# A gated-attention and Hyena block on one core: opening by quarters over three weight blocks, another order around both layer norms, the second norm's shift formed on TensorE, full-width inverse transforms

## The chip, the cores and the metric

The kernel runs on one core of a Trainium2 chip. The metric is the device time of one execution in microseconds (us): 1901.46 us, the median of three runs (1899.14 to 1902.49). Beside the runs there is one profiled execution, whose trace gives the rows shown below. About 0.2% is what separates two kernels from no difference here.

## The reference

One encoder block on x of 256 tokens by 2048 channels, in float32. Two branches (a gated linear attention in both directions, and a Hyena branch whose convolutions are done by transforms) are merged by gates, projected, and normed; a feed-forward layer and a second norm follow.

```python
proj = h @ w_in[l]
q, k, v, r, af, ab, hy_u, gate_logits = jnp.split(proj, split_idx, axis=-1)
...
merged = g[:, :, 0, :] * (y_gla @ w_gla_o[l]) + g[:, :, 1, :] * (y_hy @ w_hy_o[l])
mix = merged @ w_out[l]
h = _layernorm(DEEPNORM_ALPHA * h + mix, ln1_g[l], ln1_b[l])
ff = jnp.square(jax.nn.relu(h @ w_ff1[l])) @ w_ff2[l]
h = _layernorm(DEEPNORM_ALPHA * h + ff, ln2_g[l], ln2_b[l])
```

with, in `_layernorm`, `(xf - mu) * rsqrt(var + eps) * g + b`. In the Hyena branch each of two orders computes `zf = rfft(z)`, multiplies by the filter's spectrum, and transforms back (`irfft`).

## The kernel before, in words

**Products.** Every weight matrix is cut by the host into blocks of 128 x 2048 floats (1 MB). `fetch` (L89) issues the next block's DMA on SP's queue into one of three raw buffers and splits each half of it into a high part, cast on ACT to the reduced fp32 type `fp32r` (L81), and a low remainder, subtracted on DVE (L82). Three buffers each hold high and low halves. A product is formed from three matmuls, high by high, high by low and low by high. Where the weight stands still (`channel_pair`, L133), the activation's high and low parts lie side by side, so one matmul of 512 columns (L143) gives two of the three and one of 256 (L144) the third; sixteen such pairs make one block's product, in one of four "main" PSUM buffers, and ACT and DVE then add its two halves. Where the activation stands still (`token_products`, L162 to L164), each of the three is a matmul of 512 columns. Four "side" PSUM buffers serve all small work: filters, transforms, transposes.

**The opening.** x arrives transposed, in four pieces of 0.5 MB (`xr0` to `xr3`), and is split like a weight into `xT`. SP's queue carries, in this order, block 0's first half, two x pieces, block 0's second half, two x pieces, then block 1 by halves and the rest. TensorE runs three warm-up matmuls on zeros in plain fp32 (L209), then block 0's product `pa` (L370, L371), then the pairs of q. The constants for the filters (`filt_consts`, L233) are issued on ACT's queue. The first filter product is `mlp` (L255), also plain fp32.

**The inverse transform.** `hy_inv` (L648) runs 16 times. Into one side buffer it forms, for each of two token blocks, six matmuls of 256 columns with `mm3` (L221, matmuls L222 to L224).

**The layer norms.** z1 holds the 256 tokens as two token blocks (`tb` 0 and 1) of 128 x 2048. `norm_scale` (L758) aggregates the statistics and forms rs = rsqrt(var + eps) and nb = -mean * rs by some ten operations of one column. `norm_chunk` (L769) then does, chunk by chunk in the order of `CHUNKS` (L767), z * rs + nb on ACT (L772), times the row of scales (L773) and plus the row of shifts (L774) on DVE; the chunk at 1536 runs these two on POOL. The rows lie across all partitions and are loaded by `load_rows` (L733) on ACT's queue into one buffer, which both norms use in turn.

Before the first norm, the last quarter of the output projection is done token block by token block with `column_products` (L776), three matmuls of 256 columns at a time. After it, `turn` transposes each chunk (L824), except that the chunk at 1536 is transposed last, and splits it into `hT`. The first of ff1's products is done by token halves (`by_tile`), so that it can begin on token block 0's half: 16 half pairs of 256 and 128 columns.

The feed forward runs four quarters, `ff1(qi)` and `ff2(qi)`; `add_ff` (L848) adds the result to z1 and, in the last quarter, takes the statistics (L856). The last products are again `column_products` for token block 0, then for token block 1, each followed by the second norm and its stores: six per token block, on SP's queue (L884).

**What sets the order.** The instruction order on each engine comes from a scheduler at build time that simulates a timeline; `tc.high_priority` lifts the additions and statistics ahead of other work. Side work is queued with `later` and run by `pump` between blocks.

Of the kernel before, what the change touches and what calls it, by code (L numbers as in the profile page):

```python
# [16 lines left out]
P = 128  # L17
D = 2048
# [22 lines left out]
def block_kernel(  # L41
# [47 lines left out]
    def fetch(between=lambda n, h: None):  # L89
# [5 lines left out]
        if n > 1:  # L95
            nc.sync.dma_start(raw, wblk[n])
        parts = []
        for h in range(2):
            if n <= 1:
                hs = slice(h * D // 2, (h + 1) * D // 2)  # L100
                nc.sync.dma_start(raw[:, hs], wblk[n][:, hs])
                between(n, h)
            hi = wp.tile([P, D // 2], F32R, tag="whi", bufs=3, name=f"whi{n}_{h}")
            lo = wp.tile([P, D // 2], F32R, tag="wlo", bufs=3, name=f"wlo{n}_{h}")
            split_hi_lo(hi, lo, raw[:, h * 1024:(h + 1) * 1024])
            parts.append((hi, lo))
        queue.append(parts)

# [24 lines left out]
    def channel_pair(act, name, dst=None, scale=1.0, by_tile=False):  # L133
        if dst is None:
            dst = base.tile([P, 2, L], F32, tag="sum", name=f"{name}_s")
        for c in range(2):
            ps = psum_main(f"{name}_{c}").rearrange("p (a b) -> p a b", a=2)
            parts = next_block()
            for ts in ((slice(0, P), slice(P, L)) if by_tile and c == 0 else (slice(0, L),)):
                for kt in range(KT):  # L140
                    hi, lo = parts[kt // 8]
                    js = slice(kt % 8 * P, (kt % 8 + 1) * P)
                    MM(ps[:, :, ts], hi[:, js], act[:, kt, :, ts], start=(kt == 0), stop=False)  # L143
                    MM(ps[:, 0, ts], lo[:, js], act[:, kt, 0, ts], start=False, stop=(kt == KT - 1))  # L144
            low = base.tile([P, L], F32, tag="low", name=f"{name}_l{c}")
            nc.scalar.activation(low, ps[:, 1], AF.Copy, scale=scale)
            nc.vector.scalar_tensor_tensor(dst[:, c], ps[:, 0], scale, low, op0=ALU.mult, op1=ALU.add)
            pump()
        return dst
# [48 lines left out]
    with tc.tile_pool(name="xp", bufs=1) as xp:  # L198
        def load_x(n, h):
            for g in (2 * h, 2 * h + 1):  # L200
                xr = xp.tile([P, 4, L], F32, tag=f"xr{g}", name=f"xr{g}")
                nc.sync.dma_start(xr, xt[:, 4 * g:4 * g + 4, :])
                split_hi_lo(xT[:, 4 * g:4 * g + 4, 0], xT[:, 4 * g:4 * g + 4, 1], xr)

        wu = xp.tile([P, 512], F32, tag="wu", name="wu")
        nc.vector.memset(wu, 0.0)
        pw = psum_side("warm")
        for _ in range(3):
            MM(pw, wu[:, 0:P], wu, start=True, stop=True)  # L209
        fetch(load_x)  # L210
# [22 lines left out]
    def filt_consts():  # L233
        raw = fp.tile([P, 4, P], F32, tag="w4", name="dftraw")
        nc.scalar.dma_start(raw, dft_in)
        split_hi_lo(dfth, dftl, raw)
        mw = fp.tile([P, 3, P], F32, tag="mlpw", name="mlpw")
        nc.scalar.dma_start(mw, mlp_w)
        mc = fp.tile([P, 4], F32, tag="mlpc", name="mlpc")
        nc.scalar.dma_start(mc, mlp_c)  # L240
        et = fp.tile([P, L], F32, tag="emb", name="emb_sb")
        nc.scalar.dma_start(et, emb)
        nc.scalar.dma_start(ba_sb, ba)
        nc.scalar.dma_start(conv_sb, convp)
        nc.scalar.dma_start(mask_sb, mask_in)
        nc.scalar.dma_start(sgn_sb, sgn_in)
        nc.scalar.dma_start(ident, ident_in)
        fst["mw"], fst["mc"], fst["g"] = mw, mc, et
# [114 lines left out]
    as_sb = base.tile([P, L], F32R, tag="as", name="as_sb")  # L363
    pa = psum_main("pa").rearrange("p (a b) -> p a b", a=2)
    fetch()
    parts = next_block()
    for kt in range(KT):
        hi, lo = parts[kt // 8]
        js = slice(kt % 8 * P, (kt % 8 + 1) * P)
        MM(pa, hi[:, js], xT[:, kt], start=(kt == 0), stop=False)  # L370
        MM(pa[:, 0], lo[:, js], xT[:, kt, 0], start=False, stop=(kt == KT - 1))  # L371
# [9 lines left out]
    k_sb = qp.tile([P, 8, L], F32, tag="k", name="k_sb")  # L381
    for dst, nm, sc in ((q_sb, "q", 1.0 / 16.0), (k_sb, "k", 1.0)):
        for c2 in range(4):
            channel_pair(xT, f"{nm}{c2}", dst[:, 2 * c2:2 * c2 + 2, :], sc)
# [263 lines left out]
    def hy_inv(c, o):  # L648
        def run():
            yh, yl = cst.pop(("Y", c, o))  # L650
            py = psum_side(f"yp{c}{o}")
            for tb in range(NT):
                dst = py[:, tb * CW:(tb + 1) * CW]
                mm3(dst, dfth[:, 2], dftl[:, 2], yh[:, tb, 0], yl[:, tb, 0], True, False)
                mm3(dst, dfth[:, 3], dftl[:, 3], yh[:, tb, 1], yl[:, tb, 1], False, True)
            py3 = py.rearrange("p (a b) -> p a b", a=2)
            if o == 0:
                zf = hp.tile([P, NT, CW], F32, tag="zf", name=f"zf{c}")
                nc.vector.tensor_tensor(zf, py3, cst.pop(("x1", c)), op=ALU.mult)
# [107 lines left out]
    CHUNKS = ((0, 256), (256, 256), (1536, 512), (512, 512), (1024, 256), (1280, 256))  # L767

    def norm_chunk(z, rows, tb, at, n, rs, nb):  # L769
        zc = z[:, tb, at:at + n]  # L770
        eng = nc.gpsimd if at == 1536 else nc.vector
        nc.scalar.activation(zc, zc, AF.Identity, scale=rs, bias=nb)  # L772
        eng.tensor_tensor(zc, zc, rows[:, 0, at:at + n], op=ALU.mult)  # L773
        eng.tensor_tensor(zc, zc, rows[:, 1, at:at + n], op=ALU.add)  # L774
# [36 lines left out]
    for tb in range(NT):  # L811
# [23 lines left out]
    fts = {}  # L835

    def ff1(qi):
        f = act_tile(ep, "f", f"f{qi}") if qi % 2 == 0 else act_tile(base, "xT", f"f{qi}")
        for c2 in range(8):
            r = channel_pair(hT, f"f{qi}_{c2}", by_tile=(qi == 0 and c2 == 0))  # L840
# [7 lines left out]
    def add_ff(ps, tb, at, n, qi):  # L848
# [27 lines left out]
    for tb in range(NT):  # L876
# [135 lines left out]
```

## Time and profile before

| | us |
|---|---|
| runs, median (lowest to highest) | 1901.46 (1899.14 to 1902.49) |
| profiled execution, span | 1896.2 |
| TensorE busy | 1868.9 |
| DVE busy | 1313.3 |
| ACT busy | 949.7 |

The profile gives no time of its own for the profiled execution beside its span; the span is 5.3 us below the median of the runs. In the rows, PE is TensorE's matmuls, PEld its weight loads, DVE the VectorE, ACT the ScalarE, POOL the GpSimd, SP the queue of DMA issues; a "q" after an engine's name is its sequencer. A timeline row gives start, duration, engine, line, operation, out<-in, shapes, count, and in brackets the idle time before it with what ended it. Neighbouring matmuls overlap in the pipeline, so a matmul's price is the distance from one start to the next. In a table of windows the columns are the window, its length, then busy time and count for PE, PEld, DVE, ACT and POOL, the clock granted to TensorE (1.00 is full), the share of the DMA engines in use, and GB/s.

### The profile page before, as it was taken

The page shows a single profiled execution, that of the slowest core. Times are in us where ns is not written, and L with a number is a line of the kernel's source. Part 1 is how long each engine was busy: PE and PEld are TensorE (multiplying, and loading weights), DVE is VectorE, ACT ScalarE, POOL GpSimd, SP SyncE. Part 2 cuts the span into 40 slices and gives each one's busy share as a digit, 9 for nine tenths or more (in the row PEclk, how much of TensorE's full clock was granted, in tenths as well). Part 3 has the DMA queues.
Part 4 walks back from the last instruction along what each step waited for, and adds up shares of the span by engine and source line. Part 5 has one row for each costly group of instructions (what it writes and reads, how often), then busy time and mean ns, then how long its engine had stood idle before and what let it go on. Part 6 is the DMA issues. An engine that isn't in the chain of part 4 may idle for free.

```text
span 1896.2 us, 25333 instructions
## 1 busy us (share of the span) xinstructions
PE 1868.9 (99%) x10060; PEld 1601.9 (84%) x10060; DVE 1313.3 (69%) x1702; ACT 949.7 (50%) x1286; POOL 38.7 (2%) x60
## 2 busy tenths in 40 slices
PE   8999999999999999999999998999999999999996
PEld 7888888888888888888888888888888888888886
DVE  6888868874799888888556567666555554665456
ACT  5555556674555555555544444444434443443343
POOL 0000000000000000000000001000000000000001
PEclk9999999999999999999999999999999999999998
DMA  8667764435555555555555754555555555555552
GB/s 289 238 218 263 262 229 157 145 139 193 193 194 210 195 195 189 206 205 204 212 180 190 274 211 155 190 192 186 200 186 192 182 195 180 198 183 194 200 181 108
DMA packets 60583, 375.09 MB, mean 198 GB/s; under 512 B 7216, under 2 KB 10928, under 8 KB 20912
## 3 DMA queue, kind: packets, MB, share of 16 engines
q1 hardware_dynamic: 46512, 324.03, 47.7%
q0 software_dynamic: 5888, 29.36, 4.2%
q10 hardware_dynamic: 8064, 20.07, 3.1%
q8 instruction: 79, 1.29, 0.3%
q14 instruction: 40, 0.33, 0.0%
HBM read 356.66 MB, written 16.78 MB: 197 GB/s over the span
## 4 chain that ended last, share of the span: by engine, by line
PE 96%; DVE 2%; ACT 1%; DMA 0%; issue 0%; ACTq 0%; SPq 0%; DVEq 0%
PE f L143 12%; PE f L144 6%; PE g L143 6%; PE w L163 6%; PE w L164 6%; PE w L162 6%; PE ho L143 3%; PE go L143 3%; PE ux L143 3%; PE uv L143 3%; PE g L144 3%; PE uz L143 3%; PE ux L144 2%; PE uv L144 2%; PE uz L144 2%; PE go L144 2%
## 5 line engine op out<-in xcount | busy, mean ns | idle before, releaser
L82 DVE TENSOR_TENSOR wlo<-raw,whi 128x1024 fp32r<-128x1024 f32 x596 | 728.4, 1223 | 495.1 <-ACT whi L81 494.2
L81 ACT CAST whi<-raw 128x1024 fp32r<-128x1024 f32 x596 | 626.6, 1052 | 783.0 <-PE w L164 190.7
L143 PE MATMUL f<-hT,whi 128*128 128x512 f32 (+1 forms) x1040 | 360.2, 392 | 0.0
L144 PE MATMUL f<-hT,wlo 128*128 128x256 f32 (+1 forms) x1040 | 289.9, 279 | 0.0
L143 PEld LDWEIGHTS f<-hT,whi 128*128 128x128 f32 x1040 | 195.4, 188 | 42.9
L144 PEld LDWEIGHTS f<-hT,wlo 128*128 128x128 f32 x1040 | 197.2, 190 | 0.1
L164 PE MATMUL w<-whi,f 128*128 128x512 f32 x480 | 188.0, 392 | 0.0
L163 PE MATMUL w<-wlo,f 128*128 128x512 f32 x480 | 188.0, 392 | 0.0
L143 PE MATMUL g<-xT,whi 128*128 128x512 f32 x512 | 180.1, 393 | 0.0
L162 PE MATMUL w<-whi,f 128*128 128x512 f32 x480 | 169.2, 392 | 0.0
L144 PE MATMUL g<-xT,wlo 128*128 128x256 f32 x512 | 144.8, 283 | 0.0
L143 PEld LDWEIGHTS g<-xT,whi 128*128 128x128 f32 x512 | 96.0, 188 | 21.7
L162 PEld LDWEIGHTS w<-whi,f 128*128 128x128 f32 x480 | 90.2, 188 | 19.9
L164 PEld LDWEIGHTS w<-whi,f 128*128 128x128 f32 x480 | 90.3, 188 | 19.7
L163 PEld LDWEIGHTS w<-wlo,f 128*128 128x128 f32 x480 | 90.3, 188 | 19.6
L144 PEld LDWEIGHTS g<-xT,wlo 128*128 128x128 f32 x512 | 96.3, 188 | 0.3
L143 PE MATMUL uz<-xT,whi 128*128 128x512 f32 x256 | 91.8, 396 | 0.0
L143 PE MATMUL ux<-xT,whi 128*128 128x512 f32 x256 | 91.7, 396 | 0.0
L143 PE MATMUL go<-yg,whi 128*128 128x512 f32 x256 | 91.1, 397 | 0.0
L143 PE MATMUL uv<-xT,whi 128*128 128x512 f32 x256 | 90.7, 393 | 0.0
L143 PE MATMUL ho<-yh,whi 128*128 128x512 f32 x256 | 90.5, 399 | 0.0
L144 PE MATMUL ux<-xT,wlo 128*128 128x256 f32 x256 | 72.5, 283 | 0.0
(329 smaller groups left out, 3338.7 us busy)
## 6 DMA issues: line engine op xcount, KB each, us to landing
raw<-wblk SPq DMA_DIRECT2D x303, 1024.0 KB, 4.8
Td<-T POOLq DMA_DIRECT2D x16, 768.0 KB, 4.4
Tl<-Td POOLq DMA_DIRECT2D x16, 768.0 KB, 4.6
w<-w4s ACTq DMA_DIRECT2D x16, 512.0 KB, 4.9
zr<-ln_rows ACTq DMA_DIRECT2D x4, 1024.0 KB, 10.7
raw<-wblk SPq DMA_DIRECT2D x4, 512.0 KB, 7.0
xr<-xt SPq DMA_DIRECT2D x4, 512.0 KB, 6.3
dec<-decay_in ACTq DMA_DIRECT2D x8, 256.0 KB, 3.5
```

The source lines that it names most:

```text
L81: nc.scalar.copy(hi, src)
L82: nc.vector.tensor_tensor(lo, src, hi.bitcast(F32), op=ALU.subtract)
L143: MM(ps[:, :, ts], hi[:, js], act[:, kt, :, ts], start=(kt == 0), stop=False)
L144: MM(ps[:, 0, ts], lo[:, js], act[:, kt, 0, ts], start=False, stop=(kt == KT - 1))
L162: MM(pss[tb], sh, wh, start=(kt == 0), stop=False)
L163: MM(pss[tb], sh, wl, start=False, stop=False)
L164: MM(pss[tb], sl, wh, start=False, stop=(kt == KT - 1))
```

## The change

Six edits. `channel_pair` is cut into parts that are used one by one.

1. **Opening by quarters over three blocks.** Three main PSUM buffers are opened at once, for the gate ranks (block 0) and q's first two blocks. x's pieces go on ACT's queue (the first in two), the three blocks by quarters on SP's (block 0's first quarter in two). Quarter by quarter, the parts are split and each block's four pairs formed. The filter constants move from ACT's queue to POOL's.
2. **Full-width inverse transforms.** Six matmuls of 512 columns instead of twelve of 256.
3. **First norm.** The chunk at 1536 goes from POOL to DVE, chunks are 256, 256, 512, 512, 512 in order, and each is transposed as it is done.
4. **ff1's first pair by tokens.** Both blocks of the pair are open; for token block 0, block 0's two halves and block 1's first half (24 half pairs), then the same for token block 1, then block 1's second half at full width.
5. **Second norm.** `add_ff` multiplies by the row of scales right after the statistics. At the end a PSUM buffer gets identity times the row of shifts plus diagonal(nb) times the row of scales, two plain fp32 matmuls for each piece of 512 columns, and one DVE operation forms z * rs + that.
6. **Stores.** Four per token block instead of six.

```diff
-    def channel_pair(act, name, dst=None, scale=1.0, by_tile=False):
+    def channel_products(ps, act, half, kts, ts=FULL, opens=True):
+        hi, lo = half
+        for kt in kts:
+            js = slice(kt % 8 * P, (kt % 8 + 1) * P)
+            MM(ps[:, :, ts], hi[:, js], act[:, kt, :, ts], start=(kt == 0 and opens), stop=False)
+            MM(ps[:, 0, ts], lo[:, js], act[:, kt, 0, ts], start=False, stop=(kt == KT - 1))
...
+    def channel_pair_by_tokens(act, name):
+        dst = base.tile([P, 2, L], F32, tag="sum", name=f"{name}_s")
+        ps = [channel_psum(f"{name}_{c}") for c in range(2)]
+        blocks = [next_block() for _ in range(2)]
+        for ts in (slice(0, P), slice(P, L)):
+            for c, h in ((0, 0), (0, 1), (1, 0)):
+                channel_products(ps[c], act, blocks[c][h], range(8 * h, 8 * h + 8), ts,
+                                 opens=(c == 0 or ts.start == 0))
+        channel_products(ps[1], act, blocks[1][1], range(8, KT))
...
-        fetch(load_x)
+        for g in range(4):
+            pieces = 2 if g == 0 else 1
+            step = 4 // pieces
+            for i in range(pieces):
+                ks = slice(step * i, step * (i + 1))
+                nc.scalar.dma_start(xr[g][:, ks], xt[:, 4 * g + step * i:4 * g + step * (i + 1), :])
+            for b in range(OPENING):
+                for i in range(pieces if b == 0 else 1):
+                    w = 512 // (pieces if b == 0 else 1)
+                    cs = slice(512 * g + w * i, 512 * g + w * (i + 1))
+                    nc.sync.dma_start(raws[b][:, cs], wblk[b][:, cs])
+        for g in range(4):
+            pieces = 2 if g == 0 else 1
+            for b in range(OPENING):
+                if g % 2 == 0:
+                    halves_of[b] = weight_half(b, g // 2)
...
+                for i in range(n):
+                    at = 512 * (g % 2) + w * i
+                    cs = slice(512 * g + w * i, 512 * g + w * (i + 1))
+                    split_hi_lo(hi[:, at:at + w], lo[:, at:at + w], raws[b][:, cs])
+                    if b == 0:
+                        ks = slice(4 * g + step * i, 4 * g + step * (i + 1))
+                        split_hi_lo(xT[:, ks, 0], xT[:, ks, 1], xr[g][:, step * i:step * (i + 1)])
+                channel_products(open_ps[b], xT, halves_of[b], range(4 * g, 4 * g + 4))
...
-        nc.scalar.dma_start(raw, dft_in)
+        nc.gpsimd.dma_start(raw, dft_in)
...
-            for tb in range(NT):
-                dst = py[:, tb * CW:(tb + 1) * CW]
-                mm3(dst, dfth[:, 2], dftl[:, 2], yh[:, tb, 0], yl[:, tb, 0], True, False)
-                mm3(dst, dfth[:, 3], dftl[:, 3], yh[:, tb, 1], yl[:, tb, 1], False, True)
             py3 = py.rearrange("p (a b) -> p a b", a=2)
+            mm3(py3, dfth[:, 2], dftl[:, 2], yh[:, :, 0], yl[:, :, 0], True, False)
+            mm3(py3, dfth[:, 3], dftl[:, 3], yh[:, :, 1], yl[:, :, 1], False, True)
...
-    CHUNKS = ((0, 256), (256, 256), (1536, 512), (512, 512), (1024, 256), (1280, 256))
+    CHUNKS = ((0, 256), (256, 256), (512, 512), (1024, 512), (1536, 512))
...
-        eng = nc.gpsimd if at == 1536 else nc.vector
         nc.scalar.activation(zc, zc, AF.Identity, scale=rs, bias=nb)
-        eng.tensor_tensor(zc, zc, rows[:, 0, at:at + n], op=ALU.mult)
-        eng.tensor_tensor(zc, zc, rows[:, 1, at:at + n], op=ALU.add)
+        nc.vector.tensor_tensor(zc, zc, rows[:, 0, at:at + n], op=ALU.mult)
+        nc.vector.tensor_tensor(zc, zc, rows[:, 1, at:at + n], op=ALU.add)
...
-            if at < 1536:
-                turn(at, n)
-        turn(1536, 512)
+            turn(at, n)
...
                 nc.vector.bn_stats(st2[:, tb, at // 256 + i, :], zc[:, i * 256:(i + 1) * 256])
+            nc.vector.tensor_tensor(zc, zc, rows2[:, 0, at:at + n], op=ALU.mult)
...
-        for at, n in CHUNKS:
-            norm_chunk(z1, rows2, tb, at, n, rs, nb)
-            nc.sync.dma_start(out[tb * P:(tb + 1) * P, at:at + n], z1[:, tb, at:at + n])
+        dg = ep.tile([P, P], F32, tag="dg", bufs=2, name=f"dg{tb}")
+        nc.vector.tensor_scalar(dg, ident, nb, None, op0=ALU.mult)
+        for c in range(4):
+            at = c * 512
+            po = psum_side(f"lo{tb}{c}")
+            MM(po, ident, rows2[:, 1, at:at + 512], start=True, stop=False)
+            MM(po, dg, rows2[:, 0, at:at + 512], start=False, stop=True)
+            zc = z1[:, tb, at:at + 512]
+            nc.vector.scalar_tensor_tensor(zc, zc, rs, po, op0=ALU.mult, op1=ALU.add)
+            nc.sync.dma_start(out[tb * P:(tb + 1) * P, at:at + 512], zc)
```

More of the change, by code (lines that the diff above doesn't have):

```diff
@@ L87, in block_kernel, with fetch @@
     stop_at = [W_OUT_END - 3]
-    def fetch(between=lambda n, h: None):
+    def fetch():
         n = fetched[0]
@@ L94, in fetch @@
         raw = wp.tile([P, D], F32, tag="raw", bufs=3, name=f"raw{n}")
-        if n > 1:
-            nc.sync.dma_start(raw, wblk[n])
+        nc.sync.dma_start(raw, wblk[n])
         parts = []
         for h in range(2):
[L99 to L104, printed above, removed]
+            hi, lo = weight_half(n, h)
             split_hi_lo(hi, lo, raw[:, h * 1024:(h + 1) * 1024])
@@ L107, in fetch, with weight_half @@
         queue.append(parts)
+    def weight_half(n, h):
+        return (wp.tile([P, D // 2], F32R, tag="whi", bufs=3, name=f"whi{n}_{h}"),
+                wp.tile([P, D // 2], F32R, tag="wlo", bufs=3, name=f"wlo{n}_{h}"))
     side = []
@@ L131, in next_block, with channel_psum, channel_sum, channel_pair @@
         return queue.popleft()
-    def channel_pair(act, name, dst=None, scale=1.0, by_tile=False):
+    FULL = slice(0, L)
+    def channel_psum(name):
+        return psum_main(name).rearrange("p (a b) -> p a b", a=2)
+    def channel_products(ps, act, half, kts, ts=FULL, opens=True):
[4 more added lines that the diff above has]
+            MM(ps[:, 0, ts], lo[:, js], act[:, kt, 0, ts], start=False, stop=(kt == KT - 1))
+    def channel_sum(dst, ps, name, scale=1.0):
+        low = base.tile([P, L], F32, tag="low", name=name)
+        nc.scalar.activation(low, ps[:, 1], AF.Copy, scale=scale)
+        nc.vector.scalar_tensor_tensor(dst, ps[:, 0], scale, low, op0=ALU.mult, op1=ALU.add)
+    def channel_pair(act, name, dst=None, scale=1.0):
         if dst is None:
@@ L136, in channel_pair @@
         for c in range(2):
-            ps = psum_main(f"{name}_{c}").rearrange("p (a b) -> p a b", a=2)
+            ps = channel_psum(f"{name}_{c}")
             parts = next_block()
[L139 to L147, printed above, removed]
+            for h in range(2):
+                channel_products(ps, act, parts[h], range(8 * h, 8 * h + 8))
+            channel_sum(dst[:, c], ps, f"{name}_l{c}", scale)
+            pump()
+        return dst
+    def channel_pair_by_tokens(act, name):
[7 more added lines that the diff above has]
+        channel_products(ps[1], act, blocks[1][1], range(8, KT))
+        for c in range(2):
+            channel_sum(dst[:, c], ps[c], f"{name}_l{c}")
             pump()
@@ L195, in block_kernel @@
     qp = qkg.enter_context(tc.tile_pool(name="qp", bufs=1))
+    OPENING = 3
+    open_ps = [channel_psum(f"open{b}") for b in range(OPENING)]
     with tc.tile_pool(name="xp", bufs=1) as xp:
[L199 to L203, printed above, removed]
         wu = xp.tile([P, 512], F32, tag="wu", name="wu")
@@ L209, in block_kernel @@
             MM(pw, wu[:, 0:P], wu, start=True, stop=True)
-        fetch(load_x)
+        raws = [wp.tile([P, D], F32, tag="raw", bufs=3, name=f"raw{b}") for b in range(OPENING)]
+        fetched[0] = OPENING
+        xr = [xp.tile([P, 4, L], F32, tag=f"xr{g}", name=f"xr{g}") for g in range(4)]
+        halves_of = [None] * OPENING
+        for g in range(4):
[14 more added lines that the diff above has]
+                    halves_of[b] = weight_half(b, g // 2)
+                hi, lo = halves_of[b]
+                n = pieces if b == 0 else 1
+                w, step = 512 // n, 4 // n
+                for i in range(n):
[6 more added lines that the diff above has]
+                channel_products(open_ps[b], xT, halves_of[b], range(4 * g, 4 * g + 4))
     ba_sb = base.tile([P, 2, 8], F32, tag="ba", name="ba_sb")
@@ L234, in filt_consts @@
         raw = fp.tile([P, 4, P], F32, tag="w4", name="dftraw")
-        nc.scalar.dma_start(raw, dft_in)
+        nc.gpsimd.dma_start(raw, dft_in)
         split_hi_lo(dfth, dftl, raw)
         mw = fp.tile([P, 3, P], F32, tag="mlpw", name="mlpw")
-        nc.scalar.dma_start(mw, mlp_w)
+        nc.gpsimd.dma_start(mw, mlp_w)
         mc = fp.tile([P, 4], F32, tag="mlpc", name="mlpc")
-        nc.scalar.dma_start(mc, mlp_c)
+        nc.gpsimd.dma_start(mc, mlp_c)
         et = fp.tile([P, L], F32, tag="emb", name="emb_sb")
[L242 to L247, printed above, removed]
+        nc.gpsimd.dma_start(et, emb)
+        nc.gpsimd.dma_start(ba_sb, ba)
+        nc.gpsimd.dma_start(conv_sb, convp)
+        nc.gpsimd.dma_start(mask_sb, mask_in)
+        nc.gpsimd.dma_start(sgn_sb, sgn_in)
+        nc.gpsimd.dma_start(ident, ident_in)
         fst["mw"], fst["mc"], fst["g"] = mw, mc, et
@@ L363, in block_kernel @@
     as_sb = base.tile([P, L], F32R, tag="as", name="as_sb")
[L364 to L371, printed above, removed]
+    pa = open_ps[0]
     a_low = base.tile([P, L], F32, tag="low", name="a_low")
@@ L381, in block_kernel @@
     k_sb = qp.tile([P, 8, L], F32, tag="k", name="k_sb")
+    for c in range(2):
+        channel_sum(q_sb[:, c], open_ps[1 + c], f"q0_l{c}", 1.0 / 16.0)
+        pump()
+    for _ in range(2):
+        fetch()
     for dst, nm, sc in ((q_sb, "q", 1.0 / 16.0), (k_sb, "k", 1.0)):
-        for c2 in range(4):
+        for c2 in range(1 if nm == "q" else 0, 4):
             channel_pair(xT, f"{nm}{c2}", dst[:, 2 * c2:2 * c2 + 2, :], sc)
@@ L839, in ff1 @@
         for c2 in range(8):
-            r = channel_pair(hT, f"f{qi}_{c2}", by_tile=(qi == 0 and c2 == 0))
+            r = (channel_pair_by_tokens if qi == 0 and c2 == 0 else channel_pair)(hT, f"f{qi}_{c2}")
             nc.vector.scalar_tensor_tensor(r, r, 0.0, r, op0=ALU.max, op1=ALU.mult)
```

## The prediction

> **What bounds the kernel now.** I read the page's shares first, then its chain of waits.
>
> ```profile
> span 1896.2 us, 25333 instructions
> PE 1868.9 (99%) x10060; PEld 1601.9 (84%) x10060; DVE 1313.3 (69%) x1702; ACT 949.7 (50%) x1286; POOL 38.7 (2%) x60
> PE 96%; DVE 2%; ACT 1%; DMA 0%; issue 0%; ACTq 0%; SPq 0%; DVEq 0%
> ```
>
> TensorE is busy for 99% of the span and carries 96% of the chain. So time can come only from what TensorE is given to do, from the few stretches in which it waits, or from a lower clock. The list of its waits and the windows of its clock come next.
>
> ```profile
> PE ht L824 <- DVE zr L774: 5.3, 3, 3.3
> PE pa L370 <- DVE xT L82: 3.4, 1, 3.4
> ```
>
> ```profile
> 2.00:6.00 4.00, 4.00 (x6) 1.33 (x4) 0.00 (x0) 1.50 (x2) 0.00 (x0) 1.00 0.84 229
> 10.00:13.00 3.00, 2.85 (x9) 2.47 (x10) 2.54 (x3) 2.34 (x3) 0.00 (x0) 0.50 1.04 386
> 1165.00:1167.00 2.00, 0.60 (x4) 0.40 (x4) 1.61 (x5) 2.00 (x4) 0.76 (x1) 1.00 0.00 0
> 1167.00:1173.00 6.00, 2.74 (x14) 2.52 (x12) 5.78 (x10) 2.24 (x6) 2.30 (x2) 0.50 0.23 86
> 1886.00:1897.00 11.00, 0.00 (x0) 0.00 (x0) 5.12 (x9) 2.02 (x4) 3.06 (x2) 0.50 0.30 95
> ```
>
> The third number of a row is PE's busy time, the third from the end the clock granted to it. Three places hold all that the change can win: the opening, where products start late and at half clock; the first layer norm, where PE idles 1.40 us in one window and 3.26 in the next, and then works at 0.50; and the end, where PE has no work left. Every matmul added elsewhere lengthens the span by its own duration.
>
> **The opening.**
>
> ```profile
> 5.79 1.04 ACT L81 CAST whi<-raw 128x1024 fp32r<-128x1024 f32 x1 [2.36 <-DMA raw<-wblk]
> 13.33 1.05 ACT L81 CAST xT<-xr 128x1024 fp32r<-128x1024 f32 x1 [0.32 <-DMA xr<-xt]
> 10.15 0.79 PE L370 MATMUL pa<-xT,whi 128*128 128x512 f32 x1 [3.36 <-DVE xT L82]
> 13.42 0.40 PE L370 MATMUL pa<-xT,whi 128*128 128x512 f32 x1
> 13.77 0.39 PE L370 MATMUL pa<-xT,whi 128*128 128x512 f32 x1
> 27.45 0.70 PE L255 MATMUL mlp<-emb_sb,mlpw 33*128 33x256 f32 x2
> 28.07 0.39 PE L144 MATMUL q<-xT,wlo 128*128 128x256 f32 x1
> ```
>
> A weight tile's pair of products (512 and 256 columns) starts every 0.35 us at full clock (13.42 to 13.77). Before, the 48 pairs of the first three blocks start at 10.15; with 16.9 us of pairs, about 1.6 lost to the half clock and 0.62 of the filter product they end near 29.25. ACT's casts follow the landings: 0.5 MB at 5.79, 3.0 MB at 13.33, five steps of 1.5 us, so some 0.33 MB/us.
>
> After, the same 5 MB come as quarters. ACT issues the five x pieces, SP twelve weight pieces and one more, and the casts stand on ACT in the order: block 0's first quarter with x's, blocks 1 and 2 with x's second and third, block 0's second quarter, x's fourth, block 1's second quarter. In front of them on ACT stand those five issues; the filter constants leave that queue for POOL's, where the later stores of T queue behind them. The first products need only 0.25 MB to land; I put them at 8.5 us. Sixteen pairs (three first quarters, one second) last 5.6 us, to 14.2. Block 1's second quarter then stands behind the cast of x's last quarter, which asks for about 3.1 MB, so 13.5 to 14; with four splits still to pass through ACT and DVE I start it at 16.8. From there eight quarter-blocks of 1.41 us run without a wait: 16.8 + 11.3 + 0.6 = 28.7. Gain 0.5. Bounds: with no wait at all, 8.5 + 16.9 + 0.6 = 26.0, a gain of 3.2; with x and weights sharing the rate evenly, x's last quarter would be behind 4 MB and the end near 30.8, a loss of 1.6.
>
> **The inverse transforms.**
>
> ```profile
> 523.37 0.28 PE L223 MATMUL yp<-Yl,dfth 128*128 128x256 f32 x1
> 524.20 0.28 PE L224 MATMUL yp<-Yh,dftl 128*128 128x256 f32 x1
> 1851.37 0.40 PE L163 MATMUL w<-wlo,f 128*128 128x512 f32 x1
> 1852.53 0.39 PE L162 MATMUL w<-whi,f 128*128 128x512 f32 x1
> ```
>
> From the first yp row to the second are seven steps, 0.119 us each; from the first w row to the second five, 0.232 each. A call has twelve of the narrow ones (1.42 us) and will have six wide ones (1.39): 0.035 us in each of 16 calls, a gain of 0.6 (0.3 to 0.9 by the rounding of the rows).
>
> **The first layer norm.**
>
> ```profile
> 1162.90 0.34 PE L143 MATMUL f<-hT,whi 128*128 128x256 f32 x1
> 1163.14 0.33 PE L143 MATMUL f<-hT,whi 128*128 128x256 f32 x1
> 1165.00 0.92 DVE L773 TENSOR_TENSOR zr<-zr 128x256 f32<-128x256 f32 x2 [0.67 <-ACT zr L772]
> 1166.90 2.76 DVE L773 TENSOR_TENSOR zr<-zr 128x512 f32<-128x512 f32 x2 [0.32 <-ACT zr L772]
> 1169.58 0.68 DVE L774 TENSOR_TENSOR zr<-zr 128x512 f32<-128x512 f32 x1
> 1171.52 0.41 DVE L774 TENSOR_TENSOR zr<-zr 128x256 f32<-128x256 f32 x1
> ```
>
> POOL's chunk goes to DVE, which loses POOL's help but also its disturbance: the two multiplies at 1166.90 (512 and 256 columns) took 2.76 us, while a 512-column operation alone takes 0.68. DVE's work for the second token block, from 1165.00, is two small chunks (0.75 each), three of 512 (1.3 each) and about 1.9 us of splits for the transposes among them: 7.3, to 1172.3, where it ends at 1171.93 now. So the chain that feeds PE is no shorter. What changes is the cover: 24 half pairs of a token block instead of 16, at 0.235 us (1162.90 to 1163.14), fill 1.9 us more, but a half pair costs more than half of 0.352, eight of them twice 0.47 too much: PE has 0.9 us more to do. I reckon PE's idle time, 5.5 us before (the 5.3 in the list of waits and 0.2 of small gaps), at 4.25 after, with 3 us of it in one piece near 1168: gain 1.25 - 0.9 = 0.35. Whether the half clock after it stays decides the rest: 3.4 us of it cost 1.7, so the bounds are a gain of 2.1 and a loss of 1.
>
> The Trainium skill says on its page "TensorE: Matmul & The Clock Gate" (section "Part 1: The HAM clock gate (the "warmup" mystery)") that the clock is set by activity in a free-running window of 3413 ns. The 0.50 rows here fit that; by the rule a gap of 3 us may or may not fill a window, which would make this term 0.35 or 2.1.
>
> **The shift of the second norm on TensorE.** This is the term that decides. Sixteen matmuls of 512 columns in plain fp32 are added (identity by the row of shifts, a diagonal by the row of scales, for eight pieces). Nothing like them runs in the warm part; three rows bound the price.
>
> ```profile
> 1.49 5.30 PE L209 MATMUL warm<-wu 128*128 128x512 f32 x6 [1.49 <-DVE ones_sb L217]
> L255 PE MATMUL mlp<-emb_sb,mlpw x2: 376/428/480, 27.4 to 27.8; 33*128 33x256 f32 x2
> ```
>
> A plain fp32 matmul shows as two instructions (three matmuls, x6). Low end: two instructions at the fp32r step, 2 × 0.232 = 0.46. High end: the pair at 27.45 holds PE 0.62 us for 256 columns, 1.24 for 512. The first of that pair lasts 376 ns where the fp32r row of 256 columns shows 0.28: it occupies 0.119 + 0.096 = 0.215. Two make 0.43, and 512 columns 0.86; what is left of 0.62, 0.19, falls once for a group. Four matmuls thus take 4 × 0.86 + 0.19 = 3.6 us. The warm-up's price, 5.30 us for three, is twice that; its window shows a clock of 1.00, but the next products ran at 0.50, so I read it as a cold run.
>
> The Trainium skill's page "FP8 and Floating Point Precision" (section "TensorE Precision Notes") gives true FP32 four passes through the array. With the trace's 0.232 as a pass that estimate is 0.93 a matmul, 3.7 a group: it agrees with 0.86 and speaks against this change.
>
> *The first four of these matmuls* (identity, token block 0) don't stay at the end: in the changed order they stand among the products of f's second block, right behind the first norm, since the row of shifts and four free PSUM buffers are all that they ask for.
>
> ```profile
> 1170.68 0.33 ACTq L736 DMA_DIRECT2D zr<-ln_rows  x1
> 1172.02 0.33 ACTq L736 DMA_DIRECT2D zr<-ln_rows  x1
> zr<-ln_rows ACTq DMA_DIRECT2D x2, 1024.0 KB, 5.6
> ```
>
> The scales are issued at 1170.68, the shifts at 1172.02, and land 5.6 us later, so at 1177.6 by the rows; in the changed kernel their buffers come free a little earlier, and PE reaches these matmuls at 1176 to 1178: up to 1 us of waiting, I take 0.4. All later products of f queue behind it. There PE has work without a gap, so nothing covers the 3.6 us. Loss 4.0.
>
> *The end.*
>
> ```profile
> 1881.49 0.29 PE L790 MATMUL w<-wr,f 128*128 128x256 f32 x1
> 1881.82 0.42 DVE L853 TENSOR_TENSOR zr<-zr,w 128x256 f32<-128x256 f32 x1 [1.70 <-PE w L790]
> 1884.34 0.16 DVE L764 SCALAR_TENSOR_TENSOR lnb<-mv,lrs 128x1 f32<-128x1 f32 x1
> 1887.07 2.76 DVE L773 TENSOR_TENSOR zr<-zr 128x512 f32<-128x512 f32 x2 [0.32 <-ACT zr L772]
> 1890.69 0.74 DVE L774 TENSOR_TENSOR zr<-zr 128x256 f32<-128x256 f32 x2
> out<-zr SPq DMA_DIRECT2D x6, 128.0 KB, 2.6
> out<-zr SPq DMA_DIRECT2D x2, 256.0 KB, 2.8
> ```
>
> Call T the end of the last product, 1881.78. Before, DVE ends at 1891.43, T + 9.65, and the span 4.8 later. After, the diagonal group of token block 0 stands among block 1's products: the last product ends at T + 3.6. Then four identity matmuls (3.6) cover DVE's chain, 2.7 us to lnb now (1881.82 to 1884.50), plus 0.4 for the new multiply and 0.25 for the diagonal: 3.35. Then four diagonal ones, 3.45, and the last fused operation, 0.7: T + 3.6 + 3.6 + 3.45 + 0.7 = T + 11.35. Loss 1.7. SP's stores go from twelve to eight, the last of 256 KB instead of 128 (2.8 against 2.6). The new multiplies in the earlier groups cost nothing: DVE idles in the split of the weights there (69% busy); without that cover each would be 0.68.
>
> **Sum.** -0.5 - 0.6 - 0.35 + 4.0 + 1.7 = +4.25 us. The profiled execution's span, 1896.2, becomes 1900.45. It lies 5.3 below the median of the runs, 1901.46, and I keep that difference: 1905.7. About 0.2% (3.8 us) is what a measurement of this kernel can tell from no change: 1897.7 to 1905.3.
>
> **The rivals.**
>
> 1. *Both gaps close* (faster). If PE is fed from 8.5 us on (26.0, gain 3.2) and the longer cover keeps its clock up in the norm (the 5.5 us idle and 1.7 of cold clock go, less 0.9 of work: 6.3), the sum is -3.2 - 0.6 - 6.3 + 5.7 = -4.4, so 1897.1. For it: 24 half pairs last 5.6 us, longer than the longest wait of 3.3. Against: DVE's chain ends no earlier. It decides once PE's idle time in the norm falls below about 1 us.
> 2. *The hoisted four fall into a wait.* If PE would wait at their place for transposes or weights, 3.6 us go: 1902.1. For it: the norm's waits are near; against: the rows land after them.
> 3. *Plain fp32 at the 0.62 row's price.* Groups of 5.0: the hoist costs 5.4, the end T + 15.7, +6.0; with the gains of 1.45 that is +10, 1911.5. Against: that row's share that falls once.
> 4. *A starved opening*, by the even sharing above: -0.5 becomes +1.6, 1907.8. For it: two queues share one set of DMA engines that are already full (1.04 in 10 to 13).
>
> That the wide inverse transforms don't save what they say costs 0.6 and changes no case.
>
> **How the numbers follow.** My forecast has 0.48, its own range 1903 to 1908, of which two fifths lie below 1905.3. Rival 1 has 0.18, rival 2 0.16, rival 3 0.08, rival 4 0.10. Faster by over 0.2%: 0.18. Within: 0.16 + 0.19 = 0.35. Slower: 0.29 + 0.08 + 0.10 = 0.47. The range reaches to rival 1 and most of the way to rival 3: 1897 to 1910; about half of either lies outside.
>
> **What would show it.** In the changed profile: the end of the filter's first product near 28.7 and a wait of 2 to 3 us near 14 (opening); wide yp matmuls 0.23 apart; PE idle 4.25 us between 1158 and 1172 and a window at 0.50 behind; four identity matmuls near 1177 taking 3.6 us with no wait around them; and 14 us of fp32 matmuls in all, 11.35 us from T to DVE's last operation. A group that takes under 2.5 us, or a clock of 1.00 through the norm, would make the forecast wrong.

## The result and the profile after

| | us |
|---|---|
| before, six runs: median (lowest to highest) | 1900.30 (1898.41 to 1902.49) |
| after, six runs: median (lowest to highest) | 1906.55 (1904.49 to 1907.95) |
| ratio, with its 95% interval | 1.0027 (1.0016 to 1.0038) |
| forecast | 1905.7, range 1897 to 1910 |
| profiled span, before and after | 1896.2 and 1902.7 |

The changed kernel is 6.25 us slower, and the forecast came within 0.9 us of the total. The way there was another one. The page's first lines and its list of TensorE's waits after:

```profile
span 1902.7 us, 25235 instructions
PE 1884.3 (99%) x10012; PEld 1604.5 (84%) x10012; DVE 1312.6 (69%) x1708; ACT 942.9 (50%) x1278; POOL 30.8 (2%) x61
```

```profile
PE g L140 <- DVE vl L82: 4.8, 1, 4.8
PE ht L869 <- DVE zr L819: 2.3, 3, 1.4
PE open L140 <- ACT whi L81: 2.0, 2, 1.7
```

TensorE is as full as before, and busy for 15.4 us more. The longest wait is new and stands in no part of the kernel that the change edits: a product g of the first merge gate (the stage after the attention) waits 4.8 us for vl, the low part of an attention head's v. The wait for the norm's chunks is down from 5.3 to 2.3 us.

To see where the time went, the same tiles are looked up in both kernels; behind the counts, each row gives the first and the last start. First before, then after:

```profile
L143 PE MATMUL ho<-yh,whi x256: 395/398/403, 977.7 to 1067.8; 128*128 128x512 f32 x128
L162 PE MATMUL w<-whi,f x480: 387/389/404, 1349.0 to 1859.1; 128*128 128x512 f32 x160
L790 PE MATMUL w<-wr,f x64: 281/285/286, 1853.8 to 1881.5; 128*128 128x256 f32 x64
```

```profile
L140 PE MATMUL ho<-yh,whi x256: 395/398/403, 983.6 to 1073.7; 128*128 128x512 f32 x128
L185 PE MATMUL w<-whi,f x480: 387/389/404, 1355.4 to 1865.8; 128*128 128x512 f32 x160
L835 PE MATMUL w<-wr,f x64: 279/281/684, 1859.7 to 1891.1; 128*128 128x256 f32 x64
```

At the first Hyena output product (ho) the changed kernel is already 5.9 us late: nearly the whole loss falls into the opening, the attention and the inverse transforms. From there to the first product of ff2 (w), which takes in the first norm and the four hoisted fp32 matmuls, it loses 0.5 us. By the last product it is 9.6 us late; from that product's start to the end of the span it then takes 11.6 us instead of 14.7, and ends 6.5 us late.

### The profile page after: what moved, and what is told of

Its sections match the earlier page's. It is cut to its first block, busy times and chain, and to the rows that moved or that the text cites. A ratio compares the mean times of both kernels' runs of the same rounds, so it can differ in the third digit from the quotient of the medians.

```text
span 1902.7 us, 25235 instructions
## 1 busy us (share of the span) xinstructions
PE 1884.3 (99%) x10012; PEld 1604.5 (84%) x10012; DVE 1312.6 (69%) x1708; ACT 942.9 (50%) x1278; POOL 30.8 (2%) x61
## 3 DMA queue, kind: packets, MB, share of 16 engines
q8 instruction: 78, 1.28, 0.3%
## 4 chain that ended last, share of the span: by engine, by line
PE 96%; DVE 2%; ACT 1%; DMA 1%; issue 0%; SPq 0%; DVEq 0%
PE f L140 12%; PE f L141 6%; PE g L140 6%; PE w L185 6%; PE w L186 6%; PE w L187 6%; PE ho L140 3%; PE go L140 3%; PE g L141 3%; PE ux L140 3%; PE uv L140 3%; PE uz L140 3%; PE ux L141 2%; PE uv L141 2%; PE uz L141 2%; PE ho L141 2%
## 5 line engine op out<-in xcount | busy, mean ns | idle before, releaser
L82 DVE TENSOR_TENSOR wlo<-raw,whi 128x1024 fp32r<-128x1024 f32 (+2 forms) x603 | 728.8, 1211 | 497.4 <-ACT whi L81 496.7
L81 ACT CAST whi<-raw 128x1024 fp32r<-128x1024 f32 (+2 forms) x603 | 626.9, 1041 | 789.0 <-PE w L187 190.3
```

The costliest lines, as they stand in the source:

```text
L81: nc.scalar.copy(hi, src)
L82: nc.vector.tensor_tensor(lo, src, hi.bitcast(F32), op=ALU.subtract)
```

## The experiments

All times are medians; a ratio is to the kernel before on the same chip, in the same rounds. Runs 1 to 4, 5 to 8 and 9 to 11 were made on three chips, where the medians of before are 1900.87, 1900.64 and 1900.94 us, so a difference in us between two groups carries some 0.3 us of that.

**1. Is the new wait the opening's doing?** The wait is read from DVE and TensorE around 380 us, after (first the timeline, then a window) and before (timeline): when the output products o of the second to last head run, and when v's low part is formed.

```profile
380.88 0.39 PE L272 MATMUL o<-vh,sth 128*128 128x512 f32 x1
387.93 1.28 DVE L82 TENSOR_TENSOR vl<-v,vh 128x512 fp32r<-128x512 f32 x2
388.67 0.80 PE L140 MATMUL g<-xT,whi 128*128 128x512 f32 x1 [4.76 <-DVE vl L82]
389.48 0.63 PE L140 MATMUL g<-xT,whi 128*128 128x512 f32 x1
```

```profile
386.00:394.00 8.00, 5.33 (x19) 4.56 (x20) 8.00 (x28) 4.29 (x12) 0.00 (x0) 0.57 0.00 0
```

```profile
375.27 0.40 PE L222 MATMUL o<-vh,sth 128*128 128x512 f32 x1
382.08 1.28 DVE L82 TENSOR_TENSOR vl<-v,vh 128x512 fp32r<-128x512 f32 x2
```

vh and vl have one buffer each, so the last head's v can't be split before the head before it has run its output products o; until then v keeps two of the four main PSUM buffers. Before, o stands among the last matmuls of the first g block, and a whole block (16 pairs of 0.35 us, 5.6 us) still follows before TensorE needs v's buffers. After, o stands among the last matmuls of the second block. TensorE reaches the third block, finds no buffer, and idles 4.76 us; behind the gap it runs at half clock (pairs 0.64 apart) until 393.2, where the records give it 1.00 again. Seven pairs take 4.6 us there instead of 2.4, which costs 2.2, and the gap 4.8: some 7 us.

The order of DVE's instructions shows which edit does this. From the attention's first gate operation to its last v, it is the same, operation by operation, in the profiles of the changed kernel and of runs 2 and 4, which have the new opening, and that of before in runs 1, 9 and 11, which have the old one. (The other runs change the attention's own code and have a third order.) Three runs test it. The first takes the opening back:

```diff
-    OPENING = 3
-    open_ps = [channel_psum(f"open{b}") for b in range(OPENING)]
...
+        fetch(load_x)
...
-        nc.gpsimd.dma_start(raw, dft_in)
+        nc.scalar.dma_start(raw, dft_in)
```

> The changed kernel with the opening and the filter constants' queue of before; the other edits stay. Theory (the wait of 4.8 us for v's split near 384 us comes from an order of work that the opening's edit alone brings about, and the half clock behind it follows from the wait): no wait over 1 us and no clock of 0.50 between 300 and 425 us, and the time falls by about 6 us against the changed kernel, to before plus 0.5 us (ratio 1.000). Rival (the prediction's own terms: the opening gains 0.5 us, the rest of the loss is the fp32 matmuls): 0.5 us above the changed kernel, ratio 1.0035.

Measured: 1901.85 us, ratio 1.0007 (0.9999 to 1.0016); no wait for vl, the clock 1.00 from 300 to 425 us (a wait of 1.3 us for y stands there, as it does in the kernel before). The theory holds. This run also has a new wait of its own, in its list of waits:

```profile
PE lo L908 <- DMA zr<-ln_rows: 2.4, 1, 2.4
```

The hoisted identity matmuls arrive here before the rows of shifts do: the wait that the prediction feared. TensorE is ready for them 4.4 us after the shifts' load was issued (1171.9 to 1176.3), in the changed kernel only 7.1 us after it (1175.9 to 1183.0), and there the wait is missing.

**2. The opening alone**, in the kernel of before:

```diff
-        fetch(load_x)
+    OPENING = 3
+    open_ps = [channel_psum(f"open{b}") for b in range(OPENING)]
...
```

> The kernel of before with the opening's edit alone. Theory: the wait of about 4.8 us for v's split and the half clock behind it are there though no norm and no transform was touched; 6.2 us above before (7 lost there, 0.5 to 1 won in the opening), ratio 1.0033. Rival (the opening gains 0.5 us and moves nothing else): ratio 0.9997.

Measured: 1906.21 us, ratio 1.0034 (1.0022 to 1.0046). Its waits and its window:

```profile
PE ht L873 <- DVE zr L823: 5.3, 3, 3.3
PE g L140 <- DVE vl L82: 4.8, 1, 4.8
```

```profile
380.00:400.00 20.00, 15.24 (x77) 12.86 (x75) 18.35 (x43) 15.23 (x31) 0.00 (x0) 0.83 0.23 74
```

The norm's wait is that of before (5.3), and the wait for vl is there in full. The opening's edit alone (the queue of the filter constants belongs to it) makes 5.3 of the 6.25 us that the whole change loses, and all the rest of the change together comes to 1 us (run 1). Which part of the opening's edit turns the order was not tried apart.

**3. The same change with the order mended.**

```diff
     def gla_gates(h):
         def run():
+            with tc.high_priority():
...
```

> The changed kernel with the gate work of each attention head lifted in the scheduler's priority, so that the second to last head's output products stand among the first merge gate block's products instead of behind its second. Theory: v's split comes early enough, the wait is under 1 us, no half clock between 300 and 425 us, 6 us below the changed kernel, ratio to before about 1.000. Rival (the wait is the price of the opening's data arriving otherwise, not of the order): the wait stays and the time is that of the changed kernel, 1.0033.

Measured: 1899.36 us, ratio 0.9989 (0.9981 to 0.9998). No wait for vl is left, and the stretch is:

```profile
380.00:400.00 20.00, 19.04 (x123) 16.60 (x122) 17.34 (x39) 13.96 (x26) 0.00 (x0) 1.00 0.33 110
```

TensorE busy 19.04 us of the 20 instead of 15.24, the clock 1.00. This run keeps the opening, its queues and its data, so the price was the order's and not the data's. 7.2 us against the changed kernel: the change without its side effect is 1.5 us faster than before.

**4. Token block 0's norm on DVE again.**

```diff
+        if tb == 0:
+            for at, n in CHUNKS:
+                norm_chunk(z1, rows2, tb, at, n, rs, nb)
+                nc.sync.dma_start(out[tb * P:(tb + 1) * P, at:at + n], z1[:, tb, at:at + n])
+        else:
...
```

> The changed kernel with the second norm of token block 0 as before on ACT and DVE (all chunks on DVE), and of token block 1 on TensorE. Theory (plain fp32 matmuls cost 0.86 us each wherever TensorE has other work, and only token block 1's identity group is hidden): eight matmuls less, 6.9 us below the changed kernel, ratio to before 0.9998, with the wait near 384 us still in it. Rival (DVE's work for token block 0 gets in the way of token block 1's additions at the end): 2 to 4 us of the 6.9 come back, ratio 1.0010 to 1.0020.

Measured: 1905.11 us, ratio 1.0026 (1.0017 to 1.0036); 1.4 us won instead of 6.9. Neither theory. The run's TensorE rows tell why:

```profile
1185.67 3.60 PE L937 MATMUL lo<-zr,ident 128*128 128x512 f32 x8
1893.98 3.70 PE L938 MATMUL lo<-zr,dg 128*128 128x512 f32 x8 [3.43 <-DVE dg L933]
```

With the four side PSUM buffers free, the scheduler now hoists block 1's identity matmuls to the place behind the first norm. There they cost the same 3.4 us; and at the end the 3.43 us that they would have covered are an open wait. Of the intended saving only one group's 3.4 us is left (block 0's diagonals). Why no more than 1.4 was measured isn't settled; a wait of 1.2 us for a filter's T near 128 us, which the changed kernel's profile doesn't have, may be part of it.

**5. The same with an identity that can't come early**, gates lifted:

```diff
+        if tb == 0:
+            one = ep.tile([P, 1], F32, tag="one", name="one")
+            nc.vector.tensor_scalar(one, rs, 0.0, 1.0, op0=ALU.mult, op1=ALU.add)
+            late = ep.tile([P, P], F32, tag="late", name="late")
+            nc.vector.tensor_scalar(late, ident, one, None, op0=ALU.mult)
...
-            MM(po, ident, rows2[:, 1, at:at + 512], start=True, stop=False)
...
+                MM(po, late, rows2[:, 1, at:at + 512], start=True, stop=False)
```

> Gates lifted as in the third run; second norm of token block 0 on ACT and DVE; of token block 1 on TensorE with an identity that is multiplied by an exact one made from token block 0's scale, so that its four matmuls can't be placed before the last products. Theory (in the run before, those four were placed behind the first norm, cost 3.4 us there and left a wait of 3.4 us at the end uncovered): eight plain fp32 matmuls less than in the third run and no wait for the diagonal, 6.9 us below the third run, ratio to before 0.9953. Rival (DVE's work for token block 0 delays token block 1's statistics at the end): at least 2 us of that come back, ratio over 0.9963.

Measured: 1894.63 us, ratio 0.9967 (0.9956 to 0.9979): faster than both kernels, 4.7 us under run 3 and 2.2 less than expected. The end is as planned, identity matmuls from 1882.02 and the diagonals right behind, without a wait:

```profile
1882.02 3.60 PE L943 MATMUL lo<-zr,late 128*128 128x512 f32 x8
1885.61 3.70 PE L944 MATMUL lo<-zr,dg 128*128 128x512 f32 x8
```

The ratio is one that the rival asked for (over 0.9963), but its delay isn't there: block 1's last addition on DVE follows its product (1.60 us idle before it). Where the missing 2 us are stays open. The wait for a filter's T near 128 us is 1.9 us here and 1.4 in run 3, and the clock is at 0.50 behind it from 128.1 to 131.5, where run 3's is 1.00; but run 3's profile has a half-clock stretch of the same length in the first norm, which this one hasn't.

**6 and 7. The two norms' edits, each taken back** in the kernel of run 3.

> Gates lifted as in the third run, second norm and stores as before. Theory (the edit costs 3.5 us for the identity group behind the first norm and 0.4 us at the end, where 3.4 us of diagonals are nearly paid by the shorter chain): 3.9 us below the third run, ratio 0.9968. By the prediction's terms (4.0 and 1.7): 5.7 us below it, 0.9959.

Run 6 (second norm and stores as before, but in the new chunks and without POOL): 1895.53 us, 0.9970 (0.9959 to 0.9982), 3.8 us under run 3, the theory's number. But that is luck: the run has a second norm without POOL, which run 9 finds 1.9 us faster than before's own, so by the theory the difference should have been 5.8. By these medians the edit costs 1.9 against before; by the profiles, one execution each, runs 3 and 6 lie 5.4 apart (1897.3 and 1891.9), which would leave 3.5 to 3.7. The intervals are too wide to choose.

> Gates lifted as in the third run, first norm, its chunks and the token order of the first feed-forward pair as before. Theory (the edit to the first norm won 2.8 us, by 3 us less idle time): 2.8 us above the third run, ratio 1.0004. By the prediction's term (0.35): 0.9991.

Run 7 (old chunks with POOL, 16 half pairs): 1903.92 us, 1.0017 (1.0007 to 1.0026), 4.6 us over run 3. The prediction's 0.35 is out, and the theory's 2.8 rather small. In run 7 POOL works in no other norm.

**8. Does the place of the identity matmuls matter?** Run 3 with the late identity for both token blocks:

> Gates lifted as in the third run, both token blocks' second norm on TensorE, with the identity made from token block 0's scale, so that block 0's four identity matmuls stand among block 1's products at the end and not behind the first norm. Theory (a plain fp32 group costs 3.4 us wherever TensorE has other work, so its place doesn't matter): the time of the third run, ratio 0.9989 within 0.0006. Rival (the place behind the first norm costs more, a wait for the rows and a stall of the products queued behind): 1 to 2 us below the third run, 0.9979 to 0.9984.

Measured: 1900.74 us, 0.9999 (0.9990 to 1.0008): 1.4 us over run 3, outside the theory's 0.0006, with intervals that overlap. The rival, that hoisting is the dearer place, has nothing for it. Between "no difference" and "hoisting is the cheaper place" these runs don't decide.

**9. POOL's share of the end.** The kernel of before, second norm alone:

```diff
...
-        for at, n in CHUNKS:
-            norm_chunk(z1, rows2, tb, at, n, rs, nb)
+        for at, n in ((0, 256), (256, 256), (512, 512), (1024, 512), (1536, 512)):
+            norm_chunk(z1, rows2, tb, at, n, rs, nb, pool=False)
```

> The kernel of before, with the second norm in chunks of 256, 256, 512, 512, 512 and all on DVE, so that POOL does none of it; nothing else changed. Theory (at the end POOL's chunk slows DVE more than it takes off it, and this is most of what the changed kernel's end wins back): the stretch from the last product to the end of the span shrinks from 14.4 to 12.8 us, 1.6 us below before, ratio 0.9992. Rival (POOL takes real work off DVE): no change or up to 1 us above, ratio 1.0000 to 1.0005.

Measured: 1899.03 us, 0.9989 (0.9979 to 1.0000), 1.9 us under before. First POOL in the kernel before, then DVE in this run:

```profile
1886.41 1.47 POOL L773 TENSOR_TENSOR zr<-zr 128x512 f32<-128x512 f32 x1 [8.18 <-DVE zr L774]
1887.96 1.59 POOL L774 TENSOR_TENSOR zr<-zr 128x512 f32<-128x512 f32 x1
```

```profile
1889.38 1.28 DVE L773 TENSOR_TENSOR zr<-zr 128x512 f32<-128x512 f32 x2
1891.78 1.28 DVE L774 TENSOR_TENSOR zr<-zr 128x512 f32<-128x512 f32 x2
```

Without POOL two multiplies of 512 columns take 1.28 us on DVE; before, one of 512 and one of 256 took 2.76, just while POOL was at work. From the last product's end (1884.49) to the span's end (1897.2) are 12.7 us, against 14.4: one engine finishes sooner than two. (The run also puts the chunks in order and joins two of them.) The Trainium skill, page "Advanced Engine Details and Errata" (section "GPSIMD Details"), says that Pool shares a read and a write interface with DVE and conflicts with DVE instructions that have two SBUF inputs; these rows agree with it.

**10. What won in the first norm?** Run 3 with 16 half pairs instead of 24:

```diff
...
-            r = (channel_pair_by_tokens if qi == 0 and c2 == 0 else channel_pair)(hT, f"f{qi}_{c2}")
+            r = channel_pair(hT, f"f{qi}_{c2}", by_tile=(qi == 0 and c2 == 0))
```

> Gates lifted as in the third run, the first norm all on DVE and in order, but the first feed-forward pair by 16 half pairs as before. Theory (most of what the first norm's edit won is DVE's chain without POOL; the eight half pairs more give 1.9 us of cover for 0.9 us of work): 1 us above the third run, ratio 0.9994. Rival (the longer cover is what won): 3 us or more above it, ratio at least 1.0005.

Measured: 1898.89 us, 0.9991 (0.9982 to 1.0000), as run 3. Its wait for the norm is 3.9 us where run 3 has 2.3; the 1.6 us more of waiting and the work saved cancel as far as the runs can tell. The longer cover is not what won. Run 7 differs from this one in the chunks' order and POOL alone, and is 5.0 us slower: those two are what won, and were not tried apart.

**11. The old opening with the late identity.** No lifted gates; block 0 on DVE, block 1 on TensorE.

> Opening as before and no lifted gates, the other edits kept, second norm of token block 0 on ACT and DVE, of token block 1 on TensorE with the late identity of the fifth run. Theory (the order between 300 and 425 us is before's, the inverse wins 0.6, the first norm about 4, the end 2.9): 7.5 us below before, ratio 0.9961, at least as good as the fifth run. Rival (the new opening with lifted gates is worth more than 1 us): above the fifth run's ratio, over 0.9972.

Measured: 1894.73 us, 0.9960 (0.9947 to 0.9973), the theory's ratio: with run 5 the fastest of all, 6 us under before by the medians and 7.6 by the ratio. The two can't be told apart; the new opening, lifted gates included, isn't shown to be worth anything.

## Why the prediction was right, and where only its sum was

- **Bound.** "Time can come only from what TensorE is given to do, from the few stretches in which it waits, or from a lower clock": right, and all that was found is one of the three.
- **The opening, gain 0.5.** The filter's first product was forecast to end near 28.7, with three blocks done; it does:

```profile
7.01 0.72 PE L140 MATMUL open<-xT,whi 128*128 128x512 f32 x1
28.11 0.70 PE L305 MATMUL mlp<-emb_sb,mlpw 33*128 33x256 f32 x2
28.73 0.50 PE L140 MATMUL q<-xT,whi 128*128 128x512 f32 x1
```

  The first product came 1.5 us sooner than 8.5, the waits lay elsewhere (the longest, 1.7 us, before 9.87, and none of 2 us near 14), the end agrees: the fourth block starts at 28.73 and, before, at 29.35, a gain of 0.6 in these two executions. **The step that failed** is the one that stopped there: the edit was costed by its own stage, and no term was given to what a new start does to the order of work in later stages. The built order of the attention, which differed, has no line in the prediction. It costs 7.0 us by the profile and 7.2 by run 3, more than the whole change loses. Taking the opening back wins 4.7 (run 1) and adding it costs 5.3 (run 2); the opening's own gain and, in run 1, the new wait of 2.4 us have already come off these.
- **The inverse, 0.6.** In the changed kernel the matmuls start 0.23 apart, but a term of this size is under what the runs can resolve, and no run isolates it.
- **The first norm, 0.35.** Right mechanism for the clock (one half-clock stretch stays, from 1174.86 to 1178.28), wrong size. "So the chain that feeds PE is no shorter" was the failing sentence. From the shift and scale (lnb) to DVE's last addition the chain takes 7.6 us before (1164.33 to 1171.93) and 6.5 after (1169.37 to 1175.90). The sum gave DVE 7.3 us for the second token block, 1.9 of it for splits. It takes 5.9, because only 0.7 of splits stand before the last addition; the others follow it:

```profile
1170.04 0.92 DVE L818 TENSOR_TENSOR zr<-zr 128x256 f32<-128x256 f32 x2 [0.67 <-ACT zr L817]
1174.56 0.74 DVE L82 TENSOR_TENSOR hT<-ht,hT 128x256 fp32r<-128x256 f32 x2
1175.22 0.68 DVE L819 TENSOR_TENSOR zr<-zr 128x512 f32<-128x512 f32 x1
1175.82 1.34 DVE L82 TENSOR_TENSOR hT<-ht,hT 128x512 fp32r<-128x512 f32 x2
```

  Idle time was put at 4.25 us and is 2.3. The term measured 2.9 us in the profiles and 4.6 by run 7.
- **Plain fp32, 0.86 a matmul.** Right. The changed kernel's rows:

```profile
1183.03 3.60 PE L931 MATMUL lo<-zr,ident 128*128 128x512 f32 x8
1186.06 0.68 PE L141 MATMUL f<-hT,wlo 128*128 128x256 f32 x1
1882.63 3.59 PE L932 MATMUL lo<-zr,dg 128*128 128x512 f32 x8
1891.17 3.60 PE L931 MATMUL lo<-zr,ident 128*128 128x512 f32 x8
1894.77 3.70 PE L932 MATMUL lo<-zr,dg 128*128 128x512 f32 x8
```

  Four take 3.6 us from the first start to the end of the last, and 3.43 as a share of the chain. The four hoisted ones have no idle time before them: the 0.4 us of waiting for the rows wasn't paid.
- **The end, loss 1.7.** Identity, chain and diagonals came as worked out; the loss is 0.1 to 0.4: 14.4 us from the end of the last product before, 11.4 after, plus the 3.4 of block 0's diagonals (3.2 between the milestones above). Mis-sized was the stretch behind DVE's last operation, kept at 4.8 us: it is 3.4 after. The prediction carried the old stores' tail over to a kernel that has other stores.
- **The rivals.** None came true. Rival 1's clock does not stay up in the norm of the changed kernel; it does in the profiles of runs 5 and 8. The hoisted four fill no wait (rival 2); in run 1 they bring one of their own. A group costs 3.6 us, not 5.0 (rival 3), and the opening ends at 28.7, not 30.8 (rival 4).

The profiled executions give: up to ho +5.9, of which the order's 7.0 leaves -1.1 for the opening and the inverse, as much as forecast (a remainder, no measurement of its own); up to w +0.5, of which the hoisted 3.4 leaves -2.9 for the first norm; from there to the last product +3.2 (block 0's diagonals), and behind it -3.1: 6.5. The forecast's +4.25 came from +5.7 and -1.45. A missing loss of 7 us stood against 2.6 of gain that was too small in the first norm, 0.6 and 1.6 of loss too large at the hoist and the end: the total was right by cancelling. The step from the span to the median helped as well: the prediction kept 5.3 us between them, and after the change they lie 3.9 apart, 1.4 less. That the forecast came out within 0.9 us is luck.

## What to carry to other kernels

Where a scheduler builds the order, compare the built order of every stage, also of those that the edit doesn't touch: look for the products that free a buffer, and how much work stands between them and the next one that needs it. Give an engine's helper its price on the engine that it disturbs before counting what it takes off. And a matmul that "fills a gap" must be pinned to that gap, or the scheduler may place it where TensorE is full, as it did here twice.

## What the runs showed of the hardware that was not expected

In all thirteen profiles a stretch at half clock lasted 3.41 or 6.83 us, one twice the other; the only other lengths are those at the end of the kernel, where TensorE has no work left. In the first norm it was 6.83 in all four profiles with the old chunks (before, runs 2, 7 and 9, gaps up to 3.3 us); with the new ones (gaps up to 1.4 to 1.7 us) it was 3.41 in the changed kernel and in runs 1, 3, 6, 10 and 11, 6.83 in run 4, and none in runs 5 and 8, whose waits in that norm are the same 2.3 us. The gap of 4.8 us near 384 us brought 6.83 in the changed kernel and in run 2 and 3.41 in run 4.

DVE and POOL together took longer over the second norm at the end than DVE alone (run 9), by 1.7 us of 14.4.
